# Two products of one input run chunk by chunk together, with the rest of the start rearranged around them

## The chip, the cores and the metric

The kernel runs on one core of a Trainium2 chip. The metric is the device time of one execution in microseconds, the median over several runs. TensorE multiplies, VectorE, ScalarE and GpSimd work on tiles in the on-chip memory, and DMA queues (mostly SyncE's) bring data from HBM. Each engine takes its instructions in the order in which they stand in its queue; between engines, semaphores make one wait for another.

## The reference

One decoder layer on 256 tokens of width 1024, in float32:

```python
proj = x @ W_in                       # 1024 -> 416 + 3*512 columns
c_q, c_kv, k_rope, q_m, k_m, v_m = split(proj)        # 256, 128, 32, 512, 512, 512
q  = rms_norm(c_q) @ w_uq             # group A: 8 heads of 64 + 32 rotary
kv = rms_norm(c_kv) @ w_ukv           # group A: keys (64) and values (64) of 8 heads
a_out = causal_softmax(q k^T + q_pe rope(k_rope)^T) v
b_out = causal_softmax(q_m k_m^T - slope * distance) v_m    # group B: 8 heads of 64
x = layer_norm(alpha * x + concat(a_out, b_out) @ w_o)
h = causal_conv3(x @ w_up) + conv_b                  # 5632 columns
x = layer_norm(alpha * x + (silu(gate) * up) @ w_down)
```

With 256 tokens the block-sparse group B has a single block, so it is causal attention with a distance penalty.

## The kernel before

Products are made in a reduced float format, three times over for accuracy: each operand is split into a high part (a cast, ScalarE, L83) and a low part (the difference, VectorE, L84), and high x high, high x low and low x high are added in PSUM. So every weight tile costs one DMA, one cast and one difference before TensorE can use all of it. Weights pass through pools of seven raw, seven high and seven low tiles of 128 x 1024; a transfer waits until the raw tile seven loads back has been split, a cast until the products with the tile seven back are done.

The width of 1024 is cut into eight pieces `k` of 128, the 256 tokens into two tiles `t` of 128. The start of the kernel, which the change touches, goes in this order:

- Eight times: the piece of x (`xraw`, 128 KB) and the latents' weights for it (`r_wc`, 208 KB) are loaded over SyncE's queue and split (`first_load`, L124). TensorE makes the latents `pc` of both token tiles, six products of 416 columns for each piece (L182 to L184).
- The weights of group B's values (`r_wv`, 512 KB or 256 KB a load) follow and TensorE makes `pv`, six products of 512 columns for each piece (L244 to L246). Beside it run the latents' norms: squares and roots on ScalarE (L196, L197), scalings on VectorE (L199), six transposes on TensorE (`pct`, L210), a second scaling (L212), and the split of the turned latents `chl` (L213, L214). GpSimd rotates the shared key part (`rtmp` to `kr4`, L224 to L227).
- `pkr` (L266) turns the rotated key part; ScalarE copies it to `ksb` (L268), and GpSimd spreads it over the heads' keys `kT` (L270). Then `pk` and `pq` (keys and queries of the first heads of group A, from `chl`), then `pqk` (the first query pair of group B, from x, 24 products), then `sca`, the scores of the first head, which reads `kT` and the queries `qT` that VectorE makes from `pq` (L308).
- GpSimd makes the mask and the distance table at the very start (L156 to L166), zeroes three tiles and makes two penalty tables `tab` (L173).

A scheduler puts the instructions in order per engine, by their priority as written; where `tc.keep_in_program_order` is called it keeps the written order, and `issue_after` holds instructions behind another one. From the heads' loop on (L468) TensorE's order is written out, with products of later pieces as filling between the heads' steps; the later sections (`w_o`, the two norms, the feed-forward part) follow.

Of the kernel before, what the change touches and what calls it, by code (L numbers as in the profile page):

```python
# [14 lines left out]
P = 128  # L15
# [16 lines left out]
C_CHUNKS = ((0, 1), (1, 1), (2, 1), (3, 1), (4, 1), (5, 1), (6, 1), (7, 1))  # L32
V_CHUNKS = ((0, 2), (2, 2), (4, 1), (5, 1), (6, 1), (7, 1))
# [14 lines left out]
def layer_kernel(ctx: ExitStack, tc: tile.TileContext, a, out):  # L48
# [59 lines left out]
    preload(AF.Sqrt, 0)  # L108

# [11 lines left out]
    wc = {}  # L121
    KC = 2

    def first_load(k0, n):  # L124
        ks = slice(k0, k0 + n)
        i, o = k0 // KC, (k0 % KC) * NC0
        xr = xraw[:, ks, :].rearrange("p k t -> p (k t)")
# [26 lines left out]

    dist = att_pool.tile([P, 3 * P], F32, name="dist")
# [12 lines left out]
    MSC = HD ** -0.5  # L168

    def alibi(h):  # L170
        tab = attw.tile([P, 3 * P], F32, tag="tab", name=f"tab{h}")
        slope = 2.0 ** (-8.0 * (h + 1) / H)
        nc.gpsimd.tensor_scalar(tab, dist, -slope / MSC, None, op0=ALU.mult)  # L173
        return tab


    pc = [acc_tile(f"pc{t}") for t in range(NT)]
    for k in range(KT):
        hi, lo, o = wc[k]
# [7 lines left out]
    kr = att_pool.tile([P, NT, RO], F32, name="kr")
    ccn = att_pool.tile([P, 2 * NT * (QL + KVL)], F32, tag="m8a", name="ccn")
    NCC = NT * (QL + KVL)
    cn = ccn[:, :NCC].rearrange("p (t c) -> p t c", t=NT)  # L190
    junk = att_pool.tile([P, QL + KVL], F32, name="junk")
    ss = att_pool.tile([P, NT, 2], F32, name="ss")
    for t in range(NT):
        nc.scalar.copy(kr[:, t, :], pc[t][:, QL + KVL:NC0])
        for j, (o, n) in enumerate(((0, QL), (QL, KVL))):
            nc.scalar.activation(junk[:, o:o + n], pc[t][:, o:o + n], AF.Square, accum_out=ss[:, t, j:j + 1])  # L196
            root = nc.scalar.activation(ss[:, t, j:j + 1], ss[:, t, j:j + 1], AF.Sqrt, bias=epsc, scale=1.0 / n)  # L197
            nc.vector.reciprocal(ss[:, t, j:j + 1], ss[:, t, j:j + 1])
            nc.vector.tensor_scalar(cn[:, t, o:o + n], pc[t][:, o:o + n], ss[:, t, j:j + 1], None, op0=ALU.mult)  # L199
    preload(AF.Exp, 1, after=root)  # L200
    NB = (QL + KVL) // P
    cT = ccn[:, NCC:].rearrange("p (b t) -> p b t", b=NB)
    chl = att_pool.tile([P, 2, NB, S], F32R, name="chl")
    chi, clo = chl[:, 0], chl[:, 1]
    for b0 in range(0, NB, 2):
        pt = wk_tile(f"pct{b0}")
        for b in range(b0, min(b0 + 2, NB)):
            for t in range(NT):
                o = (b - b0) * S + t * P
                nc.tensor.transpose(pt[:, o:o + P], cn[:, t, b * P:(b + 1) * P], ident)  # L210
            g = qg[:, b:b + 1] if b < 2 else kvg
            nc.vector.tensor_scalar(cT[:, b, :], pt[:, (b - b0) * S:(b - b0 + 1) * S], g, None, op0=ALU.mult)  # L212
# [22 lines left out]


    pv = [acc_tile(f"pv{t}") for t in range(NT)]
    for k0, n in V_CHUNKS:
        hi, lo = load_split(a["w_v"][k0 // KC, :, (k0 % KC) * HALF:(k0 % KC + n) * HALF], n * HALF, f"wv{k0}")
        for k in range(k0, k0 + n):  # L240
            o = (k - k0) * HALF
            for t in range(NT):
                tk = slice(t * P, (t + 1) * P)
                nc.tensor.matmul(pv[t], xhi[:, k, tk], hi[:, o:o + HALF], start=(k == 0), stop=False)  # L244
                nc.tensor.matmul(pv[t], xhi[:, k, tk], lo[:, o:o + HALF], start=False, stop=False)  # L245
                nc.tensor.matmul(pv[t], xlo[:, k, tk], hi[:, o:o + HALF], start=False, stop=(k == KT - 1))  # L246
# [140 lines left out]

    def gen_qk(w, pr):
        hi, lo = load_split(a["w_qk"][w * 4 + pr], CH, f"wqk{w}{pr}")
        pp = acc_tile(f"pqk{w}{pr}")  # L390
        for k in range(KT):
            ks = slice(k * P, (k + 1) * P)
            for i, (wt, xt) in enumerate(((hi, xhi), (hi, xlo), (lo, xhi))):
                mm(pp[:, :S], wt[:, ks], xt[:, k, :], start=(k == 0 and i == 0), stop=(k == KT - 1 and i == 2))
                yield S
        if w:
            nc.scalar.copy(kb[:, pr, :], pp[:, :S])
        else:
            for j in range(2):
                rows = slice(j * HD, (j + 1) * HD)  # L400
                nc.scalar.copy(qz[rows, 2 * pr + j, :], pp[rows, :S])
# [377 lines left out]
```

## Time and profile before

| | |
|---|---|
| three runs | 314.87, 316.44, 316.51 us; median 316.44 |
| profiled execution | 315.36 us, its span 313.6 us |
| TensorE busy | 298.9 us, 95% of the span |
| VectorE, ScalarE, GpSimd busy | 227.3, 186.8, 39.6 us |
| mean granted clock of TensorE | 0.986 |

The span runs from the first to the last instruction that the profiler recorded. A matmul row gives the time from its start to its modelled end; successive matmuls overlap, so the pace of TensorE is read from the starts. The bracket at the end of a timeline row gives the idle time of that engine before it and what ended it. The granted clock is 1.00 at 2.4 GHz and 0.50 at 1.2 GHz.

### The profile page before, as it was taken

The page shows a single profiled execution, that of the slowest core. Times are in us where ns is not written, and L with a number is a line of the kernel's source. Part 1 is how long each engine was busy: PE and PEld are TensorE (multiplying, and loading weights), DVE is VectorE, ACT ScalarE, POOL GpSimd, SP SyncE. Part 2 cuts the span into 40 slices and gives each one's busy share as a digit, 9 for nine tenths or more (in the row PEclk, how much of TensorE's full clock was granted, in tenths as well). Part 3 has the DMA queues.
Part 4 walks back from the last instruction along what each step waited for, and adds up shares of the span by engine and source line. Part 5 has one row for each costly group of instructions (what it writes and reads, how often), then busy time and mean ns, then how long its engine had stood idle before and what let it go on. Part 6 is the DMA issues. An engine that isn't in the chain of part 4 may idle for free.

```text
span 313.6 us, 5492 instructions
## 1 busy us (share of the span) xinstructions
PE 298.9 (95%) x2058; PEld 277.8 (89%) x2058; DVE 227.3 (73%) x428; ACT 186.8 (60%) x347; POOL 39.6 (13%) x47
## 2 busy tenths in 40 slices
PE   6999999999999989799999999999999999999990
PEld 5978999999888779789999999999999999999990
DVE  3779886656654596999977666776677959873386
ACT  4789987676666179845655565565557746732410
POOL 8320100025210033900000000000000000000021
PEclk9799999999999999999999999999999999999996
DMA  6999955173233007467975545555555676000003
GB/s 201 305 371 364 304 201 201 69 262 139 72 135 103 32 0 257 175 203 257 313 275 202 186 165 189 200 200 173 175 190 197 215 264 201 1 2 0 2 0 134
DMA packets 17370, 54.36 MB, mean 173 GB/s; under 512 B 1952, under 2 KB 4400, under 8 KB 17344
## 3 DMA queue, kind: packets, MB, share of 16 engines
q1 hardware_dynamic: 16992, 52.92, 48.8%
q0 software_dynamic: 352, 1.09, 1.1%
q8 instruction: 16, 0.26, 0.4%
q14 instruction: 10, 0.08, 0.1%
HBM read 52.95 MB, written 1.05 MB: 172 GB/s over the span
## 4 chain that ended last, share of the span: by engine, by line
PE 87%; DVE 8%; ACT 2%; DMA 2%; issue 1%; SPq 0%; POOL 0%; DVEq 0%
PE pd L640 18%; PE ph L606 12%; PE ph L607 12%; PE ph L610 12%; PE pqk L275 7%; PE pm L275 7%; PE po L275 3%; PE pq L275 2%; PE sca L275 2%; PE scb L275 2%; DVE l_wu L84 2%; DMA r_wc<-in_w_c 2%; PE pc L182 1%; PE pv L246 1%; PE pv L245 1%; PE pv L244 1%
## 5 line engine op out<-in xcount | busy, mean ns | idle before, releaser
L607 PE MATMUL ph<-x1hi,l_wu 128*128 128x256 f32 x352 | 86.5, 284 | 2.1 <-DVE l_wu L84 2.1
L606 PE MATMUL ph<-x1hi,h_wu 128*128 128x256 f32 x352 | 86.4, 283 | 0.7 <-ACT x1hi L553 0.7
L607 PEld LDWEIGHTS ph<-x1hi,l_wu 128*128 128x128 f32 x352 | 66.7, 189 | 2.4 <-DVE l_wu L84 2.3
L606 PEld LDWEIGHTS ph<-x1hi,h_wu 128*128 128x128 f32 x352 | 66.6, 189 | 1.0 <-ACT x1hi L553 0.9
L84 DVE TENSOR_TENSOR l_wu<-r_wu,h_wu 128x1024 fp32r<-128x1024 f32 x44 | 56.0, 1272 | 13.6 <-ACT h_wu L83 13.5
L615 DVE SCALAR_TENSOR_TENSOR hc<-ph,cw,hc 128x255 f32<-128x255 f32 (+1 forms) x88 | 41.9, 480 | 27.8 <-ACT hc L613 26.6
L83 ACT CAST h_wu<-r_wu 128x1024 fp32r<-128x1024 f32 x44 | 45.7, 1044 | 14.3 <-PE pd L640 12.8
L610 PE MATMUL ph<-x1lo,h_wu 128*128 128x256 f32 x352 | 49.5, 283 | 0.0
L610 PEld LDWEIGHTS ph<-x1lo,h_wu 128*128 128x128 f32 x352 | 45.3, 190 | 0.0
L613 ACT ACTIVATE hc<-ph,cw 128x256 f32<-128x256 f32 x44 | 24.8, 563 | 29.5 <-PE ph L610 29.5
L705 POOL TENSOR_TENSOR r<-r,lnv 128x512 f32<-128x512 f32 x1 | 1.3, 1295 | 170.1 <-ACT r L704 170.1
L640 PE MATMUL pd<-l_wd,ghi 128*128 128x512 f32 (+1 forms) x80 | 20.2, 350 | 0.6 <-DVE l_wd L84 0.6
L640 PE MATMUL pd<-h_wd,ghi 128*128 128x512 f32 (+1 forms) x80 | 20.0, 348 | 0.0
L640 PE MATMUL pd<-h_wd,glo 128*128 128x512 f32 (+1 forms) x80 | 20.0, 348 | 0.0
L629 ACT CAST ghi<-gt 128x256 fp32r<-128x256 f32 x22 | 8.9, 404 | 18.0 <-DVE gt L626 18.0
L84 DVE TENSOR_TENSOR l_wd<-r_wd,h_wd 128x1024 fp32r<-128x1024 f32 x16 | 19.6, 1222 | 0.0
L275 PE MATMUL pqk<-xlo,h_wqk 128*128 128x256 f32 x64 | 19.1, 299 | 0.0
L275 PE MATMUL pqk<-xhi,l_wqk 128*128 128x256 f32 x64 | 19.1, 299 | 0.0
L275 PE MATMUL pqk<-xhi,h_wqk 128*128 128x256 f32 x64 | 19.0, 297 | 0.0
L83 ACT CAST h_wd<-r_wd 128x1024 fp32r<-128x1024 f32 x16 | 16.6, 1039 | 0.0
L640 PEld LDWEIGHTS pd<-l_wd,ghi 128*128 128x128 f32 x80 | 13.9, 189 | 3.1 <-DVE l_wd L84 1.0
L640 PEld LDWEIGHTS pd<-h_wd,glo 128*128 128x128 f32 x80 | 14.0, 188 | 2.1
(161 smaller groups left out, 582.7 us busy)
## 6 DMA issues: line engine op xcount, KB each, us to landing
r_wu<-in_w_up SPq DMA_DIRECT2D x44, 512.0 KB, 4.1
r_wd<-in_w_down SPq DMA_DIRECT2D x22, 512.0 KB, 3.3
r_wqk<-in_w_qk SPq DMA_DIRECT2D x8, 512.0 KB, 5.8
r_wo<-in_w_o SPq DMA_DIRECT2D x8, 512.0 KB, 3.3
lnv<-in_ln SPq DMA_DIRECT2D x4, 512.0 KB, 5.6
r_wc<-in_w_c SPq DMA_DIRECT2D x8, 208.0 KB, 4.7
xraw<-in_xT SPq DMA_DIRECT2D x8, 128.0 KB, 4.7
r_wv<-in_w_v SPq DMA_DIRECT2D x2, 512.0 KB, 5.8
```

Source lines behind the costliest of these rows:

```text
L83: nc.scalar.copy(hi[:, c], raw[:, c])
L84: nc.vector.tensor_sub(lo[:, c], raw[:, c], hi[:, c].bitcast(F32))
L182: nc.tensor.matmul(pc[t][:, :NC0], xhi[:, k, tk], hi[:, o:o + NC0], start=(k == 0), stop=False)
L244: nc.tensor.matmul(pv[t], xhi[:, k, tk], hi[:, o:o + HALF], start=(k == 0), stop=False)
L275: ins = nc.tensor.matmul(*args, **kw)
L606: nc.tensor.matmul(ph[:, :S], hi[:, ks], x1hi[:, k, :], start=(k == 0), stop=False)
L607: nc.tensor.matmul(ph[:, :S], lo[:, ks], x1hi[:, k, :], start=False, stop=False)
L610: nc.tensor.matmul(ph[:, :S], hi[:, ks], x1lo[:, k, :], start=False, stop=(k == KT - 1))
L613: nc.scalar.activation(hc, ph[:, :S], AF.Identity, bias=c[:, 3:4], scale=c[:, 2:3])
L615: nc.vector.scalar_tensor_tensor(hc[:, j:S], ph[:, 0:S - j], c[:, 2 - j:3 - j], hc[:, j:S], op0=ALU.mult, op1=ALU.add)
L629: nc.scalar.copy(ghi, gt)
L640: ins = nc.tensor.matmul(pd[t, o][:, :n], st[:, tk], mv[:, o:o + n], start=(f == 0 and i == 0), stop=(f == NF - 1 and i == 2))
```

## The change

Both products' weights are stored side by side, 416 + 512 columns for each piece (`w_cv`), and loaded with one transfer of 464 KB for each piece, except the first piece, which stays in two transfers, its latents' part over ScalarE's DMA queue. That first weight tile is cast on VectorE. TensorE runs latents (`c`) and values (`v`) of the pieces in a written order, `CV_ORDER`. The latents' chain behind them gets a high priority. The first query pair of group B comes before `pkr`, with a PSUM tile of another pool, and the splits of the later pairs' weights are held behind the latents' split. GpSimd makes its tables behind the rotation of the shared key part.

```diff
-C_CHUNKS = ((0, 1), (1, 1), (2, 1), (3, 1), (4, 1), (5, 1), (6, 1), (7, 1))
-V_CHUNKS = ((0, 2), (2, 2), (4, 1), (5, 1), (6, 1), (7, 1))
+CV_ORDER = "c0 v0 c1 c2 v1 c3 c4 v2 c5 c6 c7 v3 v4 v5 v6 v7"
...
-    def first_load(k0, n):
...
-        nc.sync.dma_start(xraw[:, ks, :], a["xT"][:, ks, :])
-        wr = load(a["w_c"][i, :, o:o + n * NC0], n * NC0, f"wc{k0}")
-        split(xr, n * S, f"x{k0}", xhi[:, ks, :].rearrange("p k t -> p (k t)"),
-              xlo[:, ks, :].rearrange("p k t -> p (k t)"))
-        w = split(wr, n * NC0, f"wc{k0}")
...
+    nc.sync.dma_start(xraw[:, 0, :], a["xT"][:, 0, :])
+    wr = raws.tile([P, CH], F32, tag="raw", name="r_wc0")
+    nc.scalar.dma_start(wr[:, :NC0], a["w_cv"][0, :, :NC0])
+    vr = load(a["w_cv"][0, :, NC0:], HALF, "wv0")
+    preload(AF.Sqrt, 0)
...
+    nc.vector.tensor_copy(wch[:, :NC0], wr[:, :NC0])
+    nc.scalar.copy(xhi[:, 0, :], xraw[:, 0, :])
+    nc.vector.tensor_sub(wcl[:, :NC0], wr[:, :NC0], wch[:, :NC0].bitcast(F32))
+    nc.vector.tensor_sub(xlo[:, 0, :], xraw[:, 0, :], xhi[:, 0, :].bitcast(F32))
+    wcv["c0"] = wch, wcl, 0
+    wcv["v0"] = *split(vr, HALF, "wv0"), 0
+    for k in range(1, KT):
+        nc.sync.dma_start(xraw[:, k, :], a["xT"][:, k, :])
+        wr = load(a["w_cv"][k], NC0 + HALF, f"wcv{k}")
+        split_x(k)
+        w = split(wr, NC0 + HALF, f"wcv{k}")
+        wcv[f"c{k}"], wcv[f"v{k}"] = (*w, 0), (*w, NC0)
...
+    pinned = True
...
+    acc = {"c": [acc_tile(f"pc{t}") for t in range(NT)], "v": [acc_tile(f"pv{t}") for t in range(NT)]}
+    pc, pv = acc["c"], acc["v"]
+    for step in CV_ORDER.split():
+        k, n = int(step[1]), NC0 if step[0] == "c" else HALF
+        hi, lo, o = wcv[step]
+        order = [(t, i) for i in range(3) for t in range(NT)] if k == 0 else [(t, i) for t in range(NT) for i in range(3)]
+        for t, i in order:
+            tk = slice(t * P, (t + 1) * P)
+            st, mv = ((xhi, hi), (xhi, lo), (xlo, hi))[i]
+            mm(acc[step[0]][t][:, :n], st[:, k, tk], mv[:, o:o + n], start=(k == 0 and i == 0),
+               stop=(k == KT - 1 and i == 2))
...
+    def gen_qk(w, pr, tile_fn=acc_tile):
+        raw = load(a["w_qk"][w * 4 + pr], CH, f"wqk{w}{pr}")
+        with ExitStack() as order:
+            for ins in (split_a, split_v)[:2 * (pr * 2 + w >= EARLY)]:
+                order.enter_context(tc.issue_after(ins.ins))
+            hi, lo = split(raw, CH, f"wqk{w}{pr}")
+        pp = tile_fn(f"pqk{w}{pr}")
...
+    with tc.high_priority():
+        for t in range(NT):
+            nc.scalar.copy(kr[:, t, :], pc[t][:, QL + KVL:NC0])
...
+                tc.keep_in_program_order(nc.tensor.transpose(pt[:, o:o + P], cn[:, t, b * P:(b + 1) * P], ident))
...
+        split_a = nc.scalar.copy(chi, cT)
+        split_v = nc.vector.tensor_sub(clo, cT, chi.bitcast(F32))
+    for i in range(EARLY):
+        run(gen_qk(i % 2, i // 2, wk_tile))
+    pinned = False
...
+    rotated = nc.gpsimd.tensor_copy(kr4, krr.to_broadcast([P, NT, 4, RO]))
...
+    late_pool = ExitStack()
+    late_pool.enter_context(tc.issue_after(rotated.ins))
     dist = att_pool.tile([P, 3 * P], F32, name="dist")
...
+    for j in range(2):
+        nc.gpsimd.memset(qz[(1 - j) * HD:(2 - j) * HD, j::2, :], 0.0)
+    late_pool.close()
...
-    for i in range(EARLY):
-        run(gen_qk(i % 2, i // 2))
     pinned = True
     heads = [Head(i) for i in range(2 * H)]
```

TensorE at the start, before: the first two pieces of the latents (`pc`, one tile per token tile).

```order
L182 MATMUL pc_201<-h_wc_104,xhi 128x416
L182 MATMUL pc_202<-h_wc_104,xhi 128x416
L183 MATMUL pc_201<-l_wc_105,xhi 128x416
L184 MATMUL pc_201<-h_wc_104,xlo 128x416
L183 MATMUL pc_202<-l_wc_105,xhi 128x416
L184 MATMUL pc_202<-h_wc_104,xlo 128x416
L182 MATMUL pc_201<-h_wc_113,xhi 128x416
```

TensorE at the start, now: from the first piece's values (`pv`) to the second piece's latents.

```order
L171 MATMUL pc_190<-h_wc_104,xlo 128x416
L171 MATMUL pc_191<-h_wc_104,xlo 128x416
L171 MATMUL pv_192<-h_wv_110,xhi 128x512
L171 MATMUL pv_193<-h_wv_110,xhi 128x512
L171 MATMUL pv_192<-l_wv_111,xhi 128x512
L171 MATMUL pv_193<-l_wv_111,xhi 128x512
L171 MATMUL pv_192<-h_wv_110,xlo 128x512
L171 MATMUL pv_193<-h_wv_110,xlo 128x512
L171 MATMUL pc_190<-h_wcv_119,xhi 128x416
L171 MATMUL pc_190<-l_wcv_120,xhi 128x416
```

Six value products stand between the first and the second piece of the latents, and the second piece reads a tile that holds both weights.

TensorE before the first scores, before: from the last value product on. `pkr` is the rotated key part, `pk` and `pq` read the latents, `pqk` is the query pair of group B.

```order
L246 MATMUL pv_303<-h_wv_378,xlo 128x512
L266 MATMUL pkr<-ident,kr_290 128x128 x2
L275 MATMUL pk_426<-chl,h_wukv 128x256
...
L275 MATMUL pq_435<-chl,h_wuq_402 128x256
L275 MATMUL pqk_455<-xhi,h_wqk_451 128x256
...
L275 MATMUL pqk_455<-xhi,l_wqk_452 128x256
L275 MATMUL sca_482<-kT,qT 128x128
```

The same place now.

```order
L171 MATMUL pv_193<-h_wcv_173,xlo 128x512
L240 MATMUL pct_316<-ident,ccn 128x128 x4
L240 MATMUL pct_323<-ident,ccn 128x128 x2
L171 MATMUL pqk_335<-xhi,h_wqk_331 128x256
...
L171 MATMUL pqk_335<-xhi,l_wqk_332 128x256
L309 MATMUL pkr<-ident,kr_364 128x128 x2
L171 MATMUL pk_429<-chl,h_wukv 128x256
...
L171 MATMUL pq_438<-chl,h_wuq_409 128x256
L171 MATMUL sca_452<-kT,qT 128x128
```

The transposes now follow all value products, and the query pair has moved from behind `pq` to ahead of `pkr`.

ScalarE around `ksb`, before: `chl` is the cast of the turned latents, `h_wqk` casts of weights of group B.

```order
L213 CAST chl<-ccn 128x768
L83 CAST h_wukv<-r_wukv 128x1024
L83 CAST h_wqk_451<-r_wqk_449 128x1024
L248 COPY v_b<-pv_302 128x4x2x64
L248 COPY v_b<-pv_303 128x4x2x64
L268 COPY ksb<-pkr 128x256
L293 COPY kT<-pk_426 64x512 x2
L83 CAST h_wqk_591<-r_wqk_589 128x1024
```

ScalarE at the same place now.

```order
L291 COPY v_b<-pv_192 128x4x2x64
L291 COPY v_b<-pv_193 128x4x2x64
L243 CAST chl<-ccn 128x768
L82 CAST h_wqk_561<-r_wqk_559 128x1024
L82 CAST h_wqk_620<-r_wqk_618 128x1024
L209 COPY qz<-pqk_335 64x256 x2
L311 COPY ksb<-pkr 128x256
L330 COPY kT<-pk_429 64x512 x2
```

Between the copies of the values and `ksb` there now stand the latents' cast, two casts of weights that are used later, and the two copies of the query pair.

## Rows read from the trace of the kernel before

**Rows 1.** The page, part 4: the chain that ended last, by engine.

```profile
PE 87%; DVE 8%; ACT 2%; DMA 2%; issue 1%; SPq 0%; POOL 0%; DVEq 0%
```

**Rows 2.** Stretches: length, busy time (instructions) by engine, granted clock, DMA share, GB/s.

```profile
0.00:3.50 3.50, 2.45 (x11) 2.45 (x12) 0.17 (x1) 1.50 (x3) 2.53 (x12) 1.00 0.40 113
3.50:5.00 1.50, 0.88 (x5) 0.48 (x3) 1.07 (x1) 0.93 (x2) 1.50 (x6) 1.00 0.72 197
5.00:7.00 2.00, 1.27 (x6) 0.67 (x4) 1.15 (x3) 0.48 (x2) 1.91 (x4) 1.00 0.97 280
...
8.00:11.00 3.00, 3.00 (x10) 2.74 (x9) 2.64 (x7) 2.55 (x7) 2.60 (x2) 0.50 0.91 283
...
16.00:20.00 4.00, 3.67 (x18) 2.81 (x17) 2.65 (x4) 3.26 (x14) 1.71 (x7) 1.00 1.07 410
28.00:34.00 6.00, 6.00 (x46) 5.68 (x45) 4.34 (x5) 5.40 (x9) 2.08 (x2) 1.00 1.01 388
```

**Rows 3.** Timeline of TensorE, first two chunks: start, length (us), instruction, [idle before].

```profile
4.60 0.64 PE L182 MATMUL pc<-h_wc,xhi 128*128 128x416 f32 x2 [0.62 <-ACT h_wc L83]
...
7.52 0.94 PE L182 MATMUL pc<-h_wc,xhi 128*128 128x416 f32 x2 [0.62 <-ACT h_wc L83]
```

**Rows 4.** Timeline of ScalarE, 3 to 8 us.

```profile
3.49 0.40 ACT L83 CAST xhi<-xraw 128x256 fp32r<-128x256 f32 x1 [1.27 <-DMA xraw<-in_xT]
...
6.93 0.54 ACT L83 CAST h_wc<-r_wc 128x416 fp32r<-128x416 f32 x1 [1.39 <-DMA r_wc<-in_w_c]
```

**Rows 5.** Tiles `xraw` and `r_wc` (min/median/max); GpSimd's timeline.

```profile
L84 DVE TENSOR_TENSOR xlo<-xraw,xhi x8: 411/416/1386, 3.9 to 13.4; 128x256 fp32r<-128x256 f32 x8
...
L84 DVE TENSOR_TENSOR l_wc<-r_wc,h_wc x8: 578/592/780, 5.2 to 14.4; 128x416 fp32r<-128x416 f32 x8
...
DMA to landing us min/median/max: 2.8/4.7/5.1
...
2.94 0.26 POOL L156 IOTA dist<- 128x128 f32 x1
...
8.05 2.68 POOL L173 TENSOR_SCALAR tab<-dist 128x384 f32<-128x384 f32 x2
...
19.04 0.40 POOL L227 COPY kr<-krr 128x256 f32<-128x256 f32 x1
```

**Rows 6.** Timeline of TensorE, 16 to 35 us.

```profile
15.99 0.54 PE L182 MATMUL pc<-h_wc,xhi 128*128 128x416 f32 x2
...
17.13 0.62 PE L244 MATMUL pv<-h_wv,xhi 128*128 128x512 f32 x2
...
28.19 0.39 PE L244 MATMUL pv<-h_wv,xhi 128*128 128x512 f32 x1
...
29.55 0.38 PE L266 MATMUL pkr<-ident,kr 128*128 128x128 f32 x2
...
31.88 0.28 PE L275 MATMUL pqk<-xhi,h_wqk 128*128 128x256 f32 x1
...
34.74 0.60 PE L275 MATMUL sca<-kT,qT 128*128 128x128 f32 x3
```

**Rows 7.** Timelines of VectorE, ScalarE and GpSimd, 22 to 37 us.

```profile
22.41 0.47 DVE L212 TENSOR_SCALAR ccn<-pct,vecs 128x256 f32<-128x256 f32 x1
...
32.08 0.69 DVE L308 TENSOR_TENSOR qT<-pq,qtab 128x512 f32<-128x512 f32 x1 [1.47 <-PE pq L275]
...
25.94 0.83 ACT L213 CAST chl<-ccn 128x768 fp32r<-128x768 f32 x1
...
30.23 0.38 ACT L268 COPY ksb<-pkr 128x256 f32<-128x256 f32 x1
...
31.89 3.98 ACT L83 CAST h_wqk<-r_wqk 128x1024 fp32r<-128x1024 f32 x4
...
35.89 0.75 ACT L401 COPY qz<-pqk 64x256 f32<-64x256 f32 x2
...
30.73 1.04 POOL L270 COPY kT<-ksb 64x1024 f32<-64x1024 f32 x1 [11.29 <-DVE l_wqk L84]
```

More of the change, by code (lines that the diff above doesn't have):

```diff
@@ new lines, in layer_kernel @@
+    qz = att_pool.tile([P, H, S], F32, name="qz")
+    kb = att_pool.tile([P, H // 2, S], F32, name="kb")
+    def gen_qk(w, pr, tile_fn=acc_tile):
[5 more added lines that the diff above has]
+        pp = tile_fn(f"pqk{w}{pr}")
+        for k in range(KT):
+            ks = slice(k * P, (k + 1) * P)
+            for i, (wt, xt) in enumerate(((hi, xhi), (hi, xlo), (lo, xhi))):
+                mm(pp[:, :S], wt[:, ks], xt[:, k, :], start=(k == 0 and i == 0), stop=(k == KT - 1 and i == 2))
+                yield S
+        if w:
+            nc.scalar.copy(kb[:, pr, :], pp[:, :S])
+        else:
+            for j in range(2):
+                rows = slice(j * HD, (j + 1) * HD)
+                nc.scalar.copy(qz[rows, 2 * pr + j, :], pp[rows, :S])
@@ new lines, in run @@
+    def run(gen):
+        for _ in gen:
+            pass
+    kr = att_pool.tile([P, NT, RO], F32, name="kr")
+    ccn = att_pool.tile([P, 2 * NT * (QL + KVL)], F32, tag="m8a", name="ccn")
+    NCC = NT * (QL + KVL)
+    cn = ccn[:, :NCC].rearrange("p (t c) -> p t c", t=NT)
+    junk = att_pool.tile([P, QL + KVL], F32, name="junk")
+    ss = att_pool.tile([P, NT, 2], F32, name="ss")
+    with tc.high_priority():
+        for t in range(NT):
+            nc.scalar.copy(kr[:, t, :], pc[t][:, QL + KVL:NC0])
+            for j, (o, n) in enumerate(((0, QL), (QL, KVL))):
+                nc.scalar.activation(junk[:, o:o + n], pc[t][:, o:o + n], AF.Square, accum_out=ss[:, t, j:j + 1])
+                root = nc.scalar.activation(ss[:, t, j:j + 1], ss[:, t, j:j + 1], AF.Sqrt, bias=epsc, scale=1.0 / n)
+                nc.vector.reciprocal(ss[:, t, j:j + 1], ss[:, t, j:j + 1])
+                nc.vector.tensor_scalar(cn[:, t, o:o + n], pc[t][:, o:o + n], ss[:, t, j:j + 1], None, op0=ALU.mult)
+        preload(AF.Exp, 1, after=root)
+        NB = (QL + KVL) // P
+        cT = ccn[:, NCC:].rearrange("p (b t) -> p b t", b=NB)
+        chl = att_pool.tile([P, 2, NB, S], F32R, name="chl")
+        chi, clo = chl[:, 0], chl[:, 1]
+        for b0 in range(0, NB, 2):
+            pt = wk_tile(f"pct{b0}")
+            for b in range(b0, min(b0 + 2, NB)):
+                for t in range(NT):
+                    o = (b - b0) * S + t * P
+                    tc.keep_in_program_order(nc.tensor.transpose(pt[:, o:o + P], cn[:, t, b * P:(b + 1) * P], ident))
+                g = qg[:, b:b + 1] if b < 2 else kvg
+                nc.vector.tensor_scalar(cT[:, b, :], pt[:, (b - b0) * S:(b - b0 + 1) * S], g, None, op0=ALU.mult)
+        split_a = nc.scalar.copy(chi, cT)
+        split_v = nc.vector.tensor_sub(clo, cT, chi.bitcast(F32))
@@ new lines, in layer_kernel @@
+    for i in range(EARLY):
+        run(gen_qk(i % 2, i // 2, wk_tile))
+    pinned = False
+    hf = RO // 2
+    k1, k2 = kr[:, :, :hf], kr[:, :, hf:]
+    cos, sin = rt[:, 0], rt[:, 1]
+    rtmp = att_pool.tile([P, 4, NT, hf], F32, name="rtmp")
+    krr = att_pool.tile([P, NT, 1, RO], F32, name="krr")
+    kr4 = att_pool.tile([P, NT, 4, RO], F32, name="kr4")
+    for i, (u, v) in enumerate(((k1, cos), (k2, sin), (k1, sin), (k2, cos))):
+        nc.gpsimd.tensor_tensor(rtmp[:, i], u, v, op=ALU.mult)
@@ L187, in layer_kernel @@
[L187 to L212, printed above, removed]
@@ L234, in layer_kernel @@
         nc.gpsimd.memset(v[:, :, :, 1, :], 0.0)
[L237 to L246, printed above, removed]
+    for j in range(2):
+        nc.gpsimd.memset(qz[(1 - j) * HD:(2 - j) * HD, j::2, :], 0.0)
+    late_pool.close()
     for t in range(NT):
@@ L386, in values @@
                 finish_pair(po, self.pr + (NP if self.b else 0))
[L388 to L401, printed above, removed]
     pm = {}
```

68 lines of the change are left out of this document (16 added, 52 removed).

## The prediction

> **What bounds the kernel now.** I read the chain of waits first [rows 1]: 87% of the span is TensorE's own work, so a change is worth what it takes off TensorE's sequence, and only where TensorE waits or runs slowly. The table by stretches comes next [rows 2]. The reader is to see that from 28 to 34 us TensorE is busy all 6.00 us, and that what is lost lies before 11 us: in 3.5 to 7 us it is busy 2.15 of 3.5 us, and from 8 to 11 us it is busy all the time at a granted clock of 0.50, the 1.2 GHz level, after those gaps. The timelines of TensorE and ScalarE [rows 3, 4] give the cause: the second piece of weights, behind 688 KB in all, releases its cast at 6.93, 1.39 us after ScalarE fell idle, and TensorE's second chunk starts at 7.52 with two products in 0.94 us, where the same two take 0.54 later [rows 6]. That gap is what the change can win from. From there to the first scores at 34.74 [rows 6] TensorE has a nearly closed sequence, and the order of all engines behind that instruction is the same in both kernels. So the whole effect is read from one number: when the first scores product, `sca`, starts.
>
> **The work that stays.** Six latent products take 1.14 us (15.99 to 17.13), six value products 1.36 us (28.19 to 29.55) at full clock [rows 6]. Both kernels run eight of each.
>
> **Start, first pair.** The first weights go over ScalarE's queue and are cast on VectorE, beside the cast of x. Before, ScalarE did both in turn from 3.49 on, and the first product came at 4.60 [rows 3, 4]. The two casts side by side bring it to about 4.1. VectorE's first difference took 1.386 us where the median is 0.416 [rows 5], beside the tables that GpSimd began at 2.94 [rows 5]; with the tables later it should take the median. These gains, 0.5 and 1.0 us, I count at nothing: what hides them is the wait for the next weights. If that wait were gone, they would be worth up to 1.5.
>
> **Start, the first whole chunk.** It is now the fifth transfer: 131 + 213 + 262 + 131 + 475 = 1212 KB (of 1000 bytes) must land before its cast, where before 688 KB had to. Late bound: the bytes of [rows 2] add up to 396 KB at 3.5 us, 691 at 5 and 1251 at 7, so 1212 at 6.9; before, 688 KB had moved at 5.0 and the cast was released at 6.93, a lag of 1.9; so 8.8. Early bound: the first 344 KB had moved at 3.0 and were being cast at 4.60 - 0.54 = 4.1, a lag of 1.0 at most; the other 868 KB at the 410 GB/s of 16 to 20 us take 2.1; so 6.2. I take 7.8, nearer to the late end, since the same small transfers stand in front of it. [...]
>
> The cast of 928 columns lies between 0.54 for 416 [rows 4] and 1.0 for 1024 (four in 3.98 [rows 7]): 0.95. The difference took 0.592 for 416 [rows 5]; in the same proportion to the cast, an estimate, 1.05 for 928. With 0.2 for the hand-overs the low half is there at 7.8 + 0.95 + 1.05 + 0.2 = 10.0; one product of 0.19 can go ahead of it. So the chunks run as if from 9.8 (bounds 8.2 and 10.8). Everything before that is done by then: the first values' weights, 606 KB in all, have moved at 4.6 and with the same lag are there at 6.5, and a cast of about 0.6 and 1.36 of products end near 8.5.
>
> **Middle.** Seven chunks of both kinds are 7 x (1.14 + 1.36) = 17.5 us. Chunks of 606 KB at the 388 GB/s of 28 to 34 us [rows 2] follow each other by 1.56 us; the second is needed 1.14 after the first, a wait of 0.42, and from the third on the values between them cover it. The casts and the differences of a chunk (0.40 + 0.95 on ScalarE, 0.42 + 1.05 on VectorE [rows 4, 5]) stay under 1.56. The clock: TensorE idles from about 8.5 to 9.8 and has worked little before, as it had when the grant fell to 0.50. A grant of 0.50 for 3 us loses 1.5 us; if it begins with the idle time it costs nothing, if with the chunks 1.1 more than the wait it hides. I take 0.4 (bounds 0 and 1.1). The last value product then ends at V = 9.8 + 17.5 + 0.4 + 0.4 = 28.1 (bounds 26.1 and 29.8).
>
> **The end of the stage.** After V come six transposes (an estimate of 0.4: a value product of four times the columns takes 1.36 / 6), the 24 products of the first query pair, moved here from behind `pq` (2.86, 31.88 to 34.74), `pkr`, `pk` and `pq` with 2.33 (29.55 to 31.88) [rows 6]: TensorE reaches `sca` at V + 5.6 = 33.7, 1.0 us earlier than before. But `sca` reads the keys' rows that GpSimd spreads and the queries that VectorE makes, and the 2.86 us that covered both are now ahead of them. Before, `pkr` at 29.55 led to `ksb` at 30.23 and to GpSimd at 30.73 [rows 6, 7]; the first of its two copies, 1.04 us, the part that the first head reads, ended at 31.8, 2.9 us before it was needed. Now ScalarE has, ahead of `ksb`, the latents' cast, two casts of later weights and two copies to `qz`. Its time from V: 0.45 for the first transposes and their hand-over, three scalings of 0.47 with an overlap of about 0.1 each (1.3), the cast 0.83 less 0.1, two casts at 3.98 / 4 = 1.0 each, the copies 0.75, `ksb` 0.38, the hop to GpSimd 0.12 (30.61 to 30.73), and 1.04 for its first copy [rows 7]: V + 6.8. So `sca` starts at V + 6.85 = 34.95: TensorE waits 1.2 us where it had not waited. If ScalarE's queue were free, the queries would be late next: `pq` ends at V + 5.6, 0.2 later VectorE starts, 0.69 for the product (32.08) [rows 7]: V + 6.5, still a wait of 0.9.
>
> **GpSimd's tables** take from 2.94 to 10.73 before [rows 5], 7.8 us. They now begin when the rotated keys are copied, which before was at 19.44 [rows 5], 2.3 behind the last latent product; now that is 28.1 - 5 x 1.36 + 2.3 = 23.6. They end at 31.4, V + 3.3, ahead of `ksb` at V + 5.6. So they hold back nobody on GpSimd, and that margin moves with V. On VectorE they now meet the latents' split. There the row speaks of little: beside the two tables from 8.05 on the longest difference of weights took 0.78 where the median is 0.592 [rows 5], 0.2 us, and the split has 0.1 us to spare, so 0.1 goes to TensorE and is inside the bounds. The Trainium skill speaks against the change here ("SBUF — State Buffer", Who interferes with whom): VectorE with two SBUF inputs and GpSimd reading SBUF exclude each other for a whole instruction. The row of 0.78 agrees with a hold, but with a short one.
>
> **The sum.** `sca` moves from 34.74 to 34.95: +0.2 us against the profiled execution's 315.36 (span 313.6 and 1.8 around it), so 315.6. The runs shown are 314.87, 316.44 and 316.51, median 316.44, 1.1 above the profiled one; the four average 315.8, and on that scale the forecast is **316.0**. Its own range is -0.9 to +1.3 about that.
>
> **Rivals.** *Faster:* the first chunk lands at the early bound and the clock costs nothing. V = 26.1, `sca` 32.95, -1.8 us: 314.0. For it speak the 410 and 388 GB/s of large transfers; against it that the same front end moved 197 and 280 GB/s in 3.5 to 7 us.
> *Slower:* the stream of chunks stays at the 283 GB/s of 8 to 11 us [rows 2], when x and weights alternated as they do now. Then chunks follow each other by 2.15 us, and the last latent chunk, not TensorE, sets the pace: its low half is there at 10.0 + 6 x 2.15 = 22.9, then 0.95 for the rest of its products and 5 x 1.36 for the values left: V = 30.6, `sca` 37.5, +2.7: 318.5. It decides from a spacing of about 1.6 us on (380 GB/s), and each 0.1 above costs 0.6. Against it: those transfers were of 128 and 208 KB, the new ones are of 475.
> *The lock:* the split of the latents waits for one whole table, 1.3 us; `pk`, `pq` and the queries follow by 1.2, and `sca` comes at V + 7.8: +1.2, 317.0. This is the skill's rule of the paragraph on the tables; the row of 0.78 leaves it a small chance.
>
> **Chances.** Forecast 0.46, faster rival 0.25, slower rival 0.22, lock 0.07. A difference of 0.5%, 1.6 us, is about what a measurement of this kernel tells from none. The faster rival lies just beyond that, so 0.21 of its 0.25 counts, with 0.03 of the forecast's scatter: 0.24 faster. Slower: 0.18 of the slower rival, 0.02 of the lock, 0.02 of the forecast: 0.22. The rest, 0.54, is no change. The range goes from -1.8 to +2.2 about 315.8, with 0.4 for the scatter of runs on either side: 313.6 to 318.4; what the slower rival adds beyond is left out.
>
> **What would show it.** In the new profile: the cast of the first 928 columns released between 7 and 8.8; TensorE idle for one to two microseconds before it and closed from the third chunk on; the last value product ending near 28; `ksb` two microseconds after `pkr`; and TensorE waiting 1 to 1.5 us for GpSimd's `kT` before `sca`. The prediction is wrong if `sca` starts without that wait, if latent chunks after the second wait for a DMA, or if the stages behind `sca` change in length.

## The result and the profile after

| | before | after |
|---|---|---|
| nine runs, median | 315.83 us (314.51 to 317.22) | 318.26 us (317.09 to 319.95) |
| profiled execution, span | 315.36, 313.6 | 319.94, 318.2 |
| first score `sca` starts | 34.74 | 37.56 |
| first product of the feed-forward part | 114.6 | 117.5 |
| last `ph` product of the high parts | 292.1 | 296.1 |

The ratio is 1.0073 (95% interval 1.0048 to 1.0098): the change makes the kernel slower by 2.4 us, where +0.2 was forecast. The profiled execution of after lies 1.7 us above its median, so its rows hold something that not every run has; the experiments sort that out.

The chain that ended last, by engine, answers to [rows 1]: TensorE's own share fell from 87 to 83%.

```profile
PE 83%; DVE 8%; ACT 4%; DMA 2%; issue 1%; SPq 1%; DVEq 0%; ACTq 0%
```

ScalarE doubled its share, which says where to look. The stretches of after (columns as in [rows 2]):

```profile
5.00:7.00 2.00, 1.87 (x9) 1.43 (x10) 1.64 (x4) 1.02 (x2) 0.00 (x0) 1.00 0.94 349
...
8.00:11.00 3.00, 1.85 (x7) 1.23 (x7) 2.33 (x3) 2.21 (x5) 0.00 (x0) 1.00 1.04 384
11.00:13.00 2.00, 1.69 (x5) 1.63 (x6) 1.84 (x4) 1.73 (x3) 0.00 (x0) 0.61 1.04 383
13.00:16.00 3.00, 3.00 (x11) 2.50 (x11) 2.78 (x5) 2.31 (x5) 0.00 (x0) 0.69 1.05 388
16.00:20.00 4.00, 4.00 (x22) 3.72 (x21) 3.47 (x6) 2.85 (x4) 0.00 (x0) 1.00 1.04 403
...
28.00:34.00 6.00, 4.91 (x36) 4.36 (x35) 3.68 (x6) 3.93 (x7) 5.21 (x7) 1.00 0.74 227
```

The DMA stream is good from 5 to 20 us: 349 to 403 GB/s, where before had 280 (5 to 7 us) and 283 (8 to 11 us). The granted clock falls to 0.61 and 0.69 between 11 and 16 us. And TensorE, which had no idle time from 28 to 34 us, now idles 1.09 us there. TensorE's timeline shows each of the three:

```profile
4.86 0.61 PE L171 MATMUL pc<-h_wc,xhi 128*128 128x416 f32 x2 [0.88 <-DVE h_wc L131]
...
8.43 0.46 PE L171 MATMUL pc<-h_wcv,xhi 128*128 128x416 f32 x1 [0.43 <-ACT h_wcv L82]
9.59 0.45 PE L171 MATMUL pc<-l_wcv,xhi 128*128 128x416 f32 x1 [0.70 <-DVE l_wcv L83]
...
11.31 0.61 PE L171 MATMUL pc<-l_wcv,xhi 128*128 128x416 f32 x1 [0.32 <-DVE l_wcv L83]
11.72 0.55 PE L171 MATMUL pc<-h_wcv,xlo 128*128 128x416 f32 x1
...
29.34 0.38 PE L240 MATMUL pct<-ident,ccn 128*128 128x128 f32 x2
30.81 0.66 PE L240 MATMUL pct<-ident,ccn 128*128 128x128 f32 x4 [1.09 <-DVE ccn L242]
31.22 0.36 PE L171 MATMUL pqk<-xhi,h_wqk 128*128 128x256 f32 x1
...
34.17 0.38 PE L309 MATMUL pkr<-ident,kr 128*128 128x128 f32 x2
...
37.56 0.68 PE L171 MATMUL sca<-kT,qT 128*128 128x128 f32 x3 [0.88 <-DVE qT L345]
```

From 11.72 a product of 416 columns starts every 0.35 us instead of every 0.19: that is the pace of the lower level, 1.2 GHz. Two transposes run at 29.34, and the other four only 1.47 us later, released by VectorE's scaling `ccn`. Before `sca` there is a second wait, for the queries. Why the scaling is late stands on ScalarE (first fence) and VectorE (second):

```profile
26.66 1.28 ACT L105 ACT_TABLE_LOAD   x1
27.95 0.20 ACT L105 ACTIVATE tabs<-zero 128x1 f32<-128x1 f32 x1
28.06 1.04 ACT L82 CAST h_wukv<-r_wukv 128x1024 fp32r<-128x1024 f32 x1
...
35.60 0.37 ACT L311 COPY ksb<-pkr 128x256 f32<-128x256 f32 x1
```

ScalarE works without a pause from 22.0 to 29.1: norms, roots, three casts of later weights and this table load. VectorE then takes the low half of the last of those weights first:

```profile
29.13 1.23 DVE L83 TENSOR_TENSOR l_wukv<-r_wukv,h_wukv 128x1024 fp32r<-128x1024 f32 x1 [0.89 <-ACT h_wukv L82]
30.28 0.48 DVE L242 TENSOR_SCALAR ccn<-pct,vecs 128x256 f32<-128x256 f32 x1
...
36.72 0.69 DVE L345 TENSOR_TENSOR qT<-pq,qtab 128x512 f32<-128x512 f32 x1 [0.34 <-PE pq L171]
```

So the first scaling waits behind `l_wukv`, which waited for `h_wukv`; and the third transpose shares its PSUM tile with the two that this scaling reads.

Behind `sca` the order of every engine is the same in both kernels, and its delay of 2.8 us reaches the feed-forward part whole (2.9 at the first product there; the way to it takes 79.9 us in both). Another 1.1 us is lost in that part. GpSimd and VectorE of after, 126 to 138 us:

```profile
126.23 4.96 POOL L680 TENSOR_TENSOR r<-r,lnv 128x1024 f32<-128x1024 f32 x2 [6.75 <-DVE l_wu L83]
131.15 5.90 POOL L681 TENSOR_TENSOR r<-r,lnv 128x1024 f32<-128x1024 f32 x2
```

```profile
128.85 3.43 DVE L83 TENSOR_TENSOR l_wu<-r_wu,h_wu 128x1024 fp32r<-128x1024 f32 x1
132.20 2.62 DVE L641 TENSOR_TENSOR glo<-gt,ghi 128x256 fp32r<-128x256 f32 x1
...
135.14 2.99 DVE L83 TENSOR_TENSOR l_wd<-r_wd,h_wd 128x1024 fp32r<-128x1024 f32 x1
```

While GpSimd scales and shifts the residual, VectorE's difference of 1024 columns takes 3.0 to 3.4 us and one of 256 takes 2.6 (1.2 and 0.4 elsewhere). TensorE pays at 138.19:

```profile
138.19 1.22 PE L651 MATMUL pd<-l_wd,ghi 128*128 128x512 f32 x2 [2.37 <-DVE l_wd L83]
139.21 1.05 PE L651 MATMUL pd<-h_wd,glo 128*128 128x512 f32 x2
```

It waits 2.37 us, and two products then take 1.0 us where two take 0.46 at full clock. The granted clock of after, from 130 to 150 us:

```profile
130.00:140.00 10.00, 7.58 (x49) 6.62 (x48) 10.00 (x8) 4.52 (x6) 7.05 (x3) 0.89 0.42 146
140.00:150.00 10.00, 10.00 (x70) 9.41 (x69) 10.00 (x15) 5.86 (x11) 0.00 (x0) 0.94 0.74 253
```

Before has the same collision, but its waits there are 2.1 and 0.6 us, apart, and the clock stays at 1.00:

```profile
131.47 0.39 PE L607 MATMUL ph<-x1hi,l_wu 128*128 128x256 f32 x1 [2.08 <-DVE l_wu L84]
...
135.54 0.73 PE L640 MATMUL pd<-l_wd,ghi 128*128 128x512 f32 x2 [0.57 <-DVE l_wd L84]
```

### The profile page after: what moved, and what is told of

Its sections match the earlier page's. It is cut to its first block, busy times and chain, and to the rows that moved or that the text cites. A ratio compares the mean times of both kernels' runs of the same rounds, so it can differ in the third digit from the quotient of the medians.

```text
span 318.2 us, 5470 instructions
## 1 busy us (share of the span) xinstructions
PE 300.9 (95%) x2058; PEld 279.4 (88%) x2058; DVE 227.5 (72%) x424; ACT 185.2 (58%) x341; POOL 40.8 (13%) x47
## 3 DMA queue, kind: packets, MB, share of 16 engines
q0 software_dynamic: 352, 1.09, 1.2%
## 4 chain that ended last, share of the span: by engine, by line
PE 83%; DVE 8%; ACT 4%; DMA 2%; issue 1%; SPq 1%; DVEq 0%; ACTq 0%
PE pd L651 18%; PE ph L617 12%; PE ph L618 12%; PE ph L621 12%; PE pqk L171 7%; PE pm L171 7%; PE po L171 3%; PE pc L171 2%; DMA r_wcv<-in_w_cv 2%; PE pq L171 2%; PE sca L171 2%; PE scb L171 2%; DVE l_wu L83 2%; PE pv L171 1%; DVE l_wd L83 1%
## 5 line engine op out<-in xcount | busy, mean ns | idle before, releaser
L651 PE MATMUL pd<-l_wd,ghi 128*128 128x512 f32 (+1 forms) x80 | 20.8, 358 | 2.4 <-DVE l_wd L83 2.4
L83 DVE TENSOR_TENSOR l_wd<-r_wd,h_wd 128x1024 fp32r<-128x1024 f32 x16 | 21.3, 1333 | 0.0
L651 PEld LDWEIGHTS pd<-h_wd,ghi 128*128 128x128 f32 x80 | 14.4, 193 | 2.0
```

The lines of the kernel that those rows point to most:

```text
L83: nc.vector.tensor_sub(lo[:, c], raw[:, c], hi[:, c].bitcast(F32))
L651: ins = nc.tensor.matmul(pd[t, o][:, :n], st[:, tk], mv[:, o:o + n], start=(f == 0 and i == 0), stop=(f == NF - 1 and i == 2))
```

## The experiments

The theory from these rows: the wait between the transposes (1.1), the wait before `sca` (0.9) and the low clock at the start (about 1.6) make the loss; the rival: what is lost behind `sca`. Four edits of the start came first.

**Zero products in the first gaps.**

```diff
+        if step in GAP:             # GAP = {"v0": 3, "c1": 1}
+            keep_warm(GAP[step], f"gap{step}")
```

> The changed kernel with four products of a zero tile added on TensorE: three behind the first values, one behind the second latent chunk, where TensorE has nothing to do. Theory (the clock): the grant of 0.50 from 11.0 to 14.7 us comes from those gaps; with them filled the granted clock stays near 1.00, the last value product ends 1.6 to 1.8 us earlier than 29.34, the first scores start near 36.0 in place of 37.56, and the time falls by about 1.6 us against the changed kernel (to 316.7). Rival (the chunks are paced by their loads and casts, and the low clock is hidden under them): the last value product moves by less than 0.4 us and the time by less than 0.5.

Measured: 317.79 us, 0.5 faster than after. In its profile the granted clock reads 1.00 from 8 to 16 us, but the last value product ends at 28.65; where no product ran slowly, without this edit (below), it ends at 27.81. The pace of the products tells why: the first twelve run at that of the lower level, although the rows of the clock show no fall there.

```profile
8.93 1.05 PE L172 MATMUL pv<-h_wv,xlo 128*128 128x512 f32 x2
9.79 1.09 PE L97 MATMUL gapv<-zero 128*128 128x128 f32 x6
10.64 0.44 PE L172 MATMUL pc<-h_wcv,xhi 128*128 128x416 f32 x1
```

Two products of 512 columns take 0.86 us from start to start, where two take 0.46 at full clock. So this profile doesn't show that the edit keeps the clock up, nor does it tell what the zero products cost. In the profile of all three edits together (below), where every product runs at full pace, the last value product ends at 28.10, 0.3 to 0.4 later than in profiles without the zero products (27.73, 27.81).

**Six transposes in three PSUM tiles.**

```diff
-        for b0 in range(0, NB, 2):
+        for b0 in range(NB):
-            for b in range(b0, min(b0 + 2, NB)):
+            for b in range(b0, b0 + 1):
```

> The changed kernel with the six transposes of the latents in three PSUM tiles in place of two, so that no transpose shares a tile with one that VectorE is reading (the order of ScalarE changes with it: one cast of later weights fewer ahead of the copy of the rotated keys). Theory (the transposes wait for VectorE's first scaling, which stands behind a split of weights): TensorE's 1.1 us of idle time between the transposes goes, the first query pair starts 1.3 us earlier than 31.22, and the first scores start 1.0 to 1.5 us earlier; time 1.0 to 1.5 us less than the changed kernel (near 317.0). Rival (the split of the latents is what is late, whatever the transposes do): TensorE waits as long for the latents ahead of the first keys, and the time stays within 0.4 us.

Measured: 317.85, 0.4 faster. The six transposes run without a pause and `sca` starts at 34.85, 2.7 earlier than in the profile of after, of which the clock at the start, which did not fall here, is 1.6. But in the feed-forward part the clock falls to 0.85 between 130 and 140 us, behind the same wait of 2.4 us for `l_wd`.

**The second product of the first pair ahead of the first score.**

```diff
     run(gen_q(0))
     pinned = True
+    run(gen_qk(1, 0))
```

> The changed kernel with the 24 products of the first key pair of group B moved from the fillings of the heads' loop to the place between the first queries and the first scores, where the query pair had stood before. Theory (the first scores wait for queries and spread keys because nothing covers them): TensorE's idle time of 0.9 to 1.05 us ahead of the scores goes and the time falls by about 1.0 us (to 317.3). Rival (the wait is given back later, since the fillings have slack): no change beyond 0.3 us.

Measured: 317.84, 0.4 faster; `sca` starts without a wait, at 38.40 with 2.86 us of product moved ahead of it, and the clock falls to 0.84 between 130 and 140 us. Of the 24 runs of these two edits, seven have a mean granted clock of 0.990 to 0.992 and take 316.0 to 317.5 us, the others 0.985 to 0.987 and 317.5 to 318.4. The profiled ones are among the latter, so the fall in the feed-forward part probably hides a part of what the start gains.

**All three.**

> The three edits together: filled gaps, three PSUM tiles, covered scores. Theory: the three losses are in series on TensorE, so the gains add up, less 0.3 us that the first keys then wait for the split of the latents: 3.5 to 3.8 us less than the changed kernel, near 314.6, 1 us under the kernel before. Rival (they overlap: one wait takes the place of another): the sum of the gains falls short by more than 1 us.

Measured: 316.5 us (ratio to before 1.0018, 0.9999 to 1.0037), 1.8 faster than after, half of what was expected. The first scores wait for nothing in its profile, the six transposes run in one piece, and together the edits leave about 0.6 us to before. The expectation had counted the 1.6 us of the clock at the start into every run; that this is the missing half is argued, not shown.

**The residual's operations on VectorE.** This takes the wait at 138 us out of both kernels, so that what remains between them comes from elsewhere.

```diff
-        if f == 6:
-            for t in range(NT):
-                nc.gpsimd.tensor_tensor(r[:, t, :], r[:, t, :], lnv[:, 0, :], op=ALU.mult)
-                nc.gpsimd.tensor_tensor(r[:, t, :], r[:, t, :], lnv[:, 1, :], op=ALU.add)
+        if f in (6, 8, 10, 12):
+            t, j = (f - 6) // 4, (f - 6) // 2 % 2
+            nc.vector.tensor_tensor(r[:, t, :], r[:, t, :], lnv[:, j, :], op=(ALU.mult, ALU.add)[j])
```

In after:

> The kernel after with one edit far behind the start: the residual's scaling and shift (four 128x1024 operations on GpSimd, all behind the gate of step 6) become four 128x1024 operations on VectorE, one each behind the gates of steps 6, 8, 10 and 12. In the trace of after these four hold GpSimd from 127 to 137 us, and beside them VectorE's 128x1024 subtraction takes 3.0 to 3.4 us where it takes 1.2 elsewhere; TensorE waits 2.4 us in one piece for the low part of the first down weights, and the granted clock then falls. Theory A (the start makes the kernel slower by about 1.5 to 2, this wait and the fall behind it make the rest): the wait goes, and 2.4 to 3.5 us with it, 314.8 to 315.9. Rival B (the slow subtractions are due to the weights' DMA or to VectorE's own load, not to GpSimd): VectorE has four more operations of 1.2 us, the wait stays, 318 to 319.

In before:

> The kernel before with the same edit (residual's scaling and shift on VectorE, one operation behind each of the gates 6, 8, 10 and 12). Its trace has two waits of 2.1 and 0.6 us there. Theory A: both go, 315.9 - 2.6 = 313.3 (312.8 to 313.8); and the difference between after and before, both with this edit, tells what the start alone costs: 1.5 to 2 us if the fall of the clock behind the wait was part of the difference, 2.4 or more if the whole of it comes from the start. Rival B: no gain, 315.9 to 316.5.

Measured: after 314.05 (313.79 to 314.13), 4.2 faster than without the edit; before 311.55 (310.81 to 312.08), ratio 0.9863 (0.9839 to 0.9886), 4.3 faster. Both gains are beyond what was expected, and both kernels' waits there are gone. VectorE of before with the edit, the operations that answer to those above:

```profile
125.78 1.22 DVE L84 TENSOR_TENSOR l_wu<-r_wu,h_wu 128x1024 fp32r<-128x1024 f32 x1
126.98 0.42 DVE L630 TENSOR_TENSOR glo<-gt,ghi 128x256 fp32r<-128x256 f32 x1
...
127.85 1.22 DVE L84 TENSOR_TENSOR l_wd<-r_wd,h_wd 128x1024 fp32r<-128x1024 f32 x1
```

They take 1.22 and 0.42 us again, so GpSimd had stretched them. The Trainium skill has this ("SBUF — State Buffer", Who interferes with whom): a VectorE instruction with two SBUF inputs contends with a GpSimd instruction that reads SBUF, and the ports that they share are an exclusive lock. The trace of after agrees: GpSimd's operations end at 131.2, 134.5 and 137.05 us, and VectorE's three end 1.1, 0.3 and 1.1 us behind these, about their own length, so each had waited for the end of one. But the two kernels are still 2.5 us apart, so the rival falls as far as this place goes: none of the difference comes from it. From the first product of the feed-forward part to VectorE's last operation the profiles have 196.1 us in before, 197.2 in after, and 192.8 in both with the edit. So the collision costs 3.3 us in before, where the two waits make 2.65, and 4.4 in after, where the wait makes 2.4 and the clock up to 1.7 (0.89 and 0.94 over 10 us each); the rest, 0.6 and at least 0.3, is not shown. The medians gain more in before (4.3) because its profiled execution lies 0.5 under its median and that of before with the edit 0.5 above.

Without that disturbance the start can be read. In after with this edit the clock is 1.00 throughout the start, and the products keep full pace from the first one on:

```profile
27.81 0.38 PE L240 MATMUL pct<-ident,ccn 128*128 128x128 f32 x2
29.25 0.66 PE L240 MATMUL pct<-ident,ccn 128*128 128x128 f32 x4 [1.06 <-DVE ccn L242]
...
35.97 0.89 PE L171 MATMUL sca<-kT,qT 128*128 128x128 f32 x4 [0.88 <-DVE qT L345]
```

The last value product ends at 27.8, near the forecast of 28.1; the low clock in the profile of after had cost 1.5 us. `sca` starts at 35.97, 1.0 later than forecast, 1.2 later than before.

**The three edits of the start on this base.**

> The three edits of the start together (zero products in the first gaps, six transposes in three PSUM tiles, one head pair's product ahead of the first score), and the residual's scaling and shift on VectorE. Theory A: 316.5 - 2.4 = 314.1 (313.3 to 314.6), within 1 us of the kernel before with the same edit, on either side of it, since this run's first score, less the 2.9 us of product moved ahead of it, stands at 34.2 us against 34.7. Rival B: as without the edit, 316.5.

Measured: 312.6 (312.12 to 312.8), 1.45 faster than the base. `sca`, less the product moved ahead of it, starts at 34.4 instead of 36.0: 1.6 us. So on the quieter base a gain at the first score arrives at the end nearly whole.

**All values behind the latents.**

```diff
-CV_ORDER = "c0 v0 c1 c2 v1 c3 c4 v2 c5 c6 c7 v3 v4 v5 v6 v7"
+CV_ORDER = "c0 v0 c1 c2 c3 c4 c5 c6 c7 v1 v2 v3 v4 v5 v6 v7"
```

> The kernel after with one edit: the order of the steps. Values' products v1 to v7 all run behind the latents' c7 (v0 stays where it is). It undoes the mixing of the two products by chunk, and keeps the common loads. Theory A (the latents' norms have to share ScalarE with the weights' casts because c7 ends only at 22.4 us, and so the transposes wait for the scaling behind the l_wukv subtraction): c7 ends at 19.7 to 21, the norms are done before the last value product, the 1.1 us wait between the transposes goes, and the last value product ends at 28.7 to 30 (7 products of 1.28 us behind c7): 0.5 to 1.7 us faster than after, 316.6 to 317.8. Rival C (TensorE idles more while the chunks arrive, the granted clock falls and stays low over the stream, c7 ends as late as before): 318.3 to 319.5.

Measured: 320.28 (319.27 to 321.64), 2.0 slower than after. TensorE:

```profile
20.81 0.40 PE L171 MATMUL pv<-h_wcv,xhi 128*128 128x512 f32 x1
...
30.56 0.38 PE L240 MATMUL pct<-ident,ccn 128*128 128x128 f32 x2
31.52 0.65 PE L240 MATMUL pct<-ident,ccn 128*128 128x128 f32 x4 [0.58 <-DVE ccn L242]
```

Neither theory held. The latents end early, at 20.8, and from 10.3 us on every product runs at full pace, but seven pieces of values take 9.75 us behind them, and half of the wait between the transposes stays. VectorE is free by then:

```profile
30.98 0.48 DVE L242 TENSOR_SCALAR ccn<-pct,vecs 128x256 f32<-128x256 f32 x1 [0.89 <-PE pct L240]
```

It has waited 0.89 us for the first transposes, and the third one still waits 0.58 for this scaling. So by this run the shared PSUM tile alone makes about half of the wait of 1.06, and VectorE's queue the other half. Mixing the two products is worth its place: it fills the gaps between chunks with work that otherwise comes at the end.

**The first weights over SyncE's queue** (base: after with the residual on VectorE, 314.05).

```diff
-    nc.scalar.dma_start(wr[:, :NC0], a["w_cv"][0, :, :NC0])
+    nc.sync.dma_start(wr[:, :NC0], a["w_cv"][0, :, :NC0])
```

> After with the residual's scaling and shift on VectorE (the quieter base, 314.05), and the first weights loaded over SyncE's queue instead of ScalarE's. In all profiles of kernels that load over ScalarE's queue the span ends 3.5 us behind VectorE's last operation, in those of the kernel before and of before with the same edit 2.9 us, with the same stores and the same last operations. Theory A (a third DMA queue lengthens the end of the program): the span ends 2.9 us behind the last operation; the first product comes 0 to 0.5 us later, and what of it reaches the first score is hidden by the stream of chunks: 313.4 (313.2 to 313.7). Rival B (the 0.6 us at the end has another cause): the end stays at 3.5 us, 314.0 to 314.5.

And the same with all other edits:

> All edits that pay: the three of the start, the residual's scaling and shift on VectorE (together 312.6), and the first weights over SyncE's queue. Theory A: 0.65 us off the end, 311.95 (311.6 to 312.3), level with the kernel before with the residual's edit (311.55) within 0.7 us. Rival B: 312.6 to 313.

Measured: 314.18 (313.96 to 315.62) and 312.25 (312.2 to 312.35): no gain on the base, 0.35 us with all the edits. VectorE's last operation and the span, for the base, for the base with this edit, and for before with the residual on VectorE:

```profile
core 0 of [0], span 312.2 us
...
307.84 0.88 DVE L700 SCALAR_TENSOR_TENSOR r<-r,lnst,lnv 128x256 f32<-128x256 f32 x2
```

```profile
core 0 of [0], span 312.3 us
...
308.25 0.88 DVE L700 SCALAR_TENSOR_TENSOR r<-r,lnst,lnv 128x256 f32<-128x256 f32 x2
```

```profile
core 0 of [0], span 310.3 us
...
306.57 0.88 DVE L689 SCALAR_TENSOR_TENSOR r<-r,lnst,lnv 128x256 f32<-128x256 f32 x2
```

The span ends 3.5, 3.2 and 2.9 us behind that operation. Half of the 0.6 us goes with ScalarE's queue; the other half has a cause that no run here shows. With all edits the end is 3.15 instead of 3.56. On the base, the later landing of the first whole chunks takes back what the end gives: their low halves are used 0.3 and 0.4 us later, and `sca` starts 0.4 later.

**GpSimd's tables back at the start** (same base).

> The same base (314.05), and GpSimd's tables, masks and zeros back at the program's start, as the kernel before has them. Theory A (the tables hold nobody in either place): within 0.4 us of the base, 313.7 to 314.4, first score at 36.0 as in the base. Rival B (late, they collide with VectorE's scalings and subtractions between 25 and 33 us): 0.5 us or more faster, first score at 35.5 or earlier. Rival C (early, they stretch VectorE's first subtractions, 1.39 us for one of 256 columns in the trace of before): the first chunks are late by 0.5 to 1, and 314.5 to 315.

Measured: 314.77 (314.24 to 315.67), 0.7 slower. VectorE's first cast, with the tables early and in the base:

```profile
4.48 1.71 DVE L131 CAST h_wc<-r_wc 128x416 fp32r<-128x416 f32 x1 [3.49 <-DMA r_wc<-in_w_cv]
```

```profile
4.69 0.38 DVE L131 CAST h_wc<-r_wc 128x416 fp32r<-128x416 f32 x1 [3.69 <-DMA r_wc<-in_w_cv]
```

It takes 1.71 instead of 0.38 us beside GpSimd's distance table and zeros, and the first product starts at 6.33 instead of 5.21. So rival C, in its time and its direction: the tables' new place is a gain that the change needs, since it puts this cast on VectorE. How the cast's 1.3 us become 0.7 at the end is not shown: in this profile, 0.7 above its median, the products also run at the lower level's pace from 6.33 to 12.2 us, and `sca` starts 1.5 later than in the base.

**The transposes alone** (same base, three PSUM tiles).

> The same base (314.05), and the six transposes in three PSUM tiles. In the base's trace the wait between them is 1.06 us, the last value product ends at 27.8, near the 28.1 that was forecast, and the first score starts at 36.0, 1.0 us later than forecast. Theory A (the term that failed is the transposes'): the wait goes, the first score starts at 34.9 to 35.1, and 1.0 us goes with it, 313.05 (312.8 to 313.3). Rival B (the wait comes back whole in front of the first score, for the queries): first score at 36.0, 314.0.

Measured: 313.02 (312.87 to 314.68), 1.03 faster, as theory A has it. TensorE:

```profile
27.89 0.82 PE L240 MATMUL pct<-ident,ccn 128*128 128x128 f32 x6
...
35.01 0.89 PE L171 MATMUL sca<-kT,qT 128*128 128x128 f32 x4 [0.88 <-DVE qT L345]
```

The six run in one piece, and `sca` starts at 35.01, where the forecast had 34.95. That they meet this closely is chance in part: here the queries end the wait, 0.88 us, and not GpSimd's copy, as the forecast had it.

## Why the prediction was wrong

**The step that failed** is the end of the stage: "After V come six transposes (an estimate of 0.4)". They take 1.85 us from the first to the `pqk` behind them (27.81 to 29.66), 1.88 in the profile of after. Of that, 1.06 is a wait. The estimate priced the transposes and forgot what releases them: the third one shares a PSUM tile with what the first scaling reads. And I had this scaling start at V + 0.45, as if VectorE's queue were empty; but `l_wukv` stands there, held by ScalarE, whose queue I counted only from V on, and it starts at V + 0.9 (28.71). Each makes about half of the wait, by the run with all values behind the latents. Everything behind it moves: the latents' cast starts at 30.63, V + 2.8 instead of V + 1.75. The experiment on the transposes alone removes this one wait, and 1.03 us with it.

**A term that was not in the sum:** the end of the program. I took everything behind `sca` as unchanged, without a reason but the order of the engines; the span ends 0.6 us later behind the same last operation, half of it through the additional DMA queue. The feed-forward part is 1.1 us longer in the profile of after too, through the collision and the clock; in the pair without the collision it is equal.

**The clock** was mis-sized for some runs: 0.4 (bounds 0 and 1.1). In the profile of after it costs 1.5, with the same code and the clock at 1.00 it costs nothing, and the last value product ends at 27.8. Where it falls in the runs without a profile is not shown; of the nine of after, five have a mean granted clock of 0.990 or 0.991 (317.09 to 318.44 us) and four of 0.979 to 0.986 (318.26 to 319.95).

**What was right, and what only nearly.** The cast of the first 928 columns was released at 7.42 (7 to 8.8 forecast); the chunks run as if from 9.4 (9.8); the stream of chunks holds 383 GB/s and more, so the slower rival's mechanism was wrong although its time, 318.5, came out; V is 28.1 forecast, 27.8 measured with a full clock. From `pkr` to `ksb` it is 1.4 us, where two had been forecast. The wait before `sca` is 0.88 instead of 1.2 and ends on the queries (35.82 in the base), which had been named as next in line; GpSimd's first copy of `kT`, from 34.53, is done 0.1 to 0.3 us before them. The first product came later, at 4.86 instead of 4.1, and the tables' move, counted at nothing, is worth 0.7 us to the new arrangement. The lock rival's place was quiet: partly beside the tables the latents' split (`chl` on VectorE) took 0.96 us in after and in the base, where before has 0.95, and 1.21 in the run with the transposes alone.

**The sum with what was measured.** In the pair without the feed-forward collision: `sca` +1.2 (35.97 against 34.8 in before with the edit) and the end +0.6 make 1.8 of the 1.9 us between the two profiled executions (313.99 and 312.08). Between the medians it is 2.5, since the profiled execution of before with the edit lies 0.5 above its median. Against the forecast of +0.2, the failed step is 1.0 of it and the end 0.6. The front end did gain 1.7 us, where 1.45 was forecast (V at 29.55 before, 27.8 after); what stands behind it took back 3: the transposes with their wait 1.85, the wait before `sca` 0.88, and 0.2 that is not shown.

The best kernel is before with the residual's operations on VectorE: 311.55. The changed start with all edits comes to 312.25, 0.7 behind it.

## What to carry to other kernels

When an operation is moved to a place where another engine has a backlog, price what releases it, and read that engine's queue from well ahead of the moment, not from it. Transposes that share a PSUM tile with one that VectorE reads wait for VectorE: give them tiles of their own. A GpSimd operation on large tiles beside VectorE's differences is to be looked for first when VectorE's operations have two lengths: here four of them cost over 4 us by the medians, more than the change did (2.4).

## What the runs showed that I had not expected

- A load over a third DMA queue, ScalarE's, of 208 KB at the start of the program, lengthens its end by 0.3 to 0.4 us (3.48 and 3.17, 3.56 and 3.15 us with and without it).
- The same start had a granted clock of 0.61 to 0.69 from 11 to 16 us in one execution and 1.00 in another (after, and after with a later stage changed). In before the clock was 0.50 from 8 to 11 us [rows 2], in before with the residual's edit the rows give 1.00 there, and the first score started at 34.74 and 34.8: there the low clock cost nothing, since what the full clock won went into a wait for the values' weights (TensorE busy 2.77 of the 4 us from 16 to 20, where before had 3.67).
- The rows of the granted clock can miss a slow start. In nine of the fourteen profiles, that of before with the residual's edit among them (4.5 to 8.6 us), the first products start every 0.35 us for 416 columns, the pace of the lower level, while the rows read 1.00. The pace has to be read beside them.
- A cast of 128x416 on VectorE took 1.71 us beside GpSimd's distance table and zeros and 0.38 without.
